# An encoder trunk on one core: every fourth low part of the weights made by ScalarE and an accumulating GpSimd DMA

## The chip, the cores and the metric

The kernel runs on one core of a Trainium2 chip. The metric is device microseconds of one execution; the median of two runs of the kernel before is 1818.07 us (1817.77 to 1818.36).

## What is computed

The reference is a trunk of two layers over 256 tokens of width 2048, all in float32. Cut to what matters:

```python
def hybrid_layer(x, ...):                       # x: (1, 256, 2048)
    h = rms_norm(x, norm_g)
    z = jnp.einsum('bsd,de->bse', h, w_in)      # 2048 -> 14848: q, k, v, gates of three branches, merge gates
    ya = retention(rq, rk, rv, ...)             # 4 heads of 256
    yb = multiscale_pool(pv, pool_w, ...)       # windows 2, 4, 8, 16
    yc = windowed_gqa(aq, ak, av, ...)          # 8 query heads, 2 key heads of 128
    ya, yb, yc = (y * silu(gate) @ w_branch)    # each 1024 -> 2048
    merged = g0 * ya + g1 * yb + g2 * yc
    return x + jnp.einsum('bsd,de->bse', merged, w_out)   # 2048 -> 2048
```

Nearly all arithmetic is in products of 256 tokens with weight matrices, 336 MB of weights in the two layers.

## The kernel before

The weights are cut into 628 tiles of 128 partitions x 1024 float32 (512 KB). `plan` lists them in the order of their use. To keep float32 precision with the faster float32r matmul, each weight tile is split into a high part (its value rounded to float32r) and a low part (the rest), and a product is the sum of three: high by high, high by low, low by high. A tile passes through these steps:

- SP loads it from HBM into a buffer `raw` (L193, four buffers).
- ScalarE (ACT) casts it to the high part `whi` (L200, four buffers).
- VectorE (DVE) subtracts: `wlo = raw - whi` (L207, three buffers).
- TensorE (PE) reads `whi` and `wlo`: `gemm_n` (L308, activations stationary, 12 matmuls of 512 columns a tile) or `gemm_t` (L338 and L341, weights stationary).

`weights()` is called once per tile and runs the steps ahead of the use: when tile i is taken, the low parts are issued up to tile i + 2, the high parts up to i + 3, and loads up to four tiles beyond the last low part. A buffer that is still read makes the instruction that refills it wait: the low part of tile j goes into the buffer of tile j - 3, so it waits for PE's last matmul on that low part; the load of tile j + 4 goes into the buffer of tile j, so it waits until both parts of tile j are made.

Beside this, `Side` runs the smaller work (norms, attention heads, retention, pooling, merge) as generators that advance by one tick per weight tile. They use ACT and DVE for what PSUM holds, PE for small products and transposes, and GpSimd (POOL) for 16 small powers (`rsqrt`, L382). PE's accumulators of a group of tiles are two PSUM buffers in turn. Within an engine the instructions run in the order in which the scheduler put them, and a waiting instruction holds all behind it on its engine; SP's loads are such a queue too.

Of the kernel before, what the change touches and what calls it, by code (L numbers as in the profile page):

```python
# [9 lines left out]
F32 = mybir.dt.float32  # L10
F32R = mybir.dt.float32r
AF = mybir.ActivationFunctionType
# [22 lines left out]


class Side:
    """Work beside the weight loops: generators that advance by one tick per weight tile; each yields the ticks to wait."""

    def __init__(self):  # L40
        self.live = []
# [25 lines left out]


class First(Task):
    """A task made on demand, apart from the ticks."""  # L70


@with_exitstack
def kernel(
# [71 lines left out]
            yield 1  # L146
        return task.value

# [1 line left out]
    def n_tiles(mat, c0, nk):  # L150
        return [(mat[k2 * 256:(k2 + 1) * 256, c0:c0 + 512].rearrange("(k p) e -> p k e", p=P), 2, 512) for k2 in range(nk // 2)]

# [50 lines left out]
    def lo_to(n):  # L203
        while len(los) < min(n, len(plan)):
            i = len(los)
            lo = wp.tile(list(raws[i].shape), F32R, tag="wlo", name=nm("wlo"), bufs=N_LO)
            nc.vector.tensor_sub(lo, raws[i], his[i].bitcast(F32))  # L207
            los.append(lo)

    def weights():  # L210
        """the next tile of the plan, split; splits and loads of later ones run ahead."""
        i = used[0]
        used[0] += 1
        ahead = min(i, 1) if i < 6 else N_LO - 1
        hi_to(i + ahead + 1)
        lo_to(i + ahead + 1)
        load_to(len(los) + N_RAW)
        hi_to(i + ahead + (1 if ahead < N_LO - 1 else 2))
        return his[i], los[i]

# [1 line left out]
    xa = cp.tile([P, 2, D], F32, name="xa")  # L222
    xr = x.rearrange("b (t p) d -> p (b t) d", p=P)

# [59 lines left out]
        yield 1  # L284
        nc.vector.tensor_copy(cols[:, 32:48], pc[:, 0:16])

# [1 line left out]
    def split(dst_hi, dst_lo, src, scale=None):  # L288
        if scale is None:
            nc.scalar.copy(dst_hi, src)  # L290
# [3 lines left out]
            nc.vector.scalar_tensor_tensor(dst_lo, src, scale, dst_hi.bitcast(F32), ALU.mult, ALU.subtract)  # L294

    def gemm_n(act, nk, early=False):
        """act [K, tokens] in split pairs of K-tiles; returns [tokens, 512]."""
        pt = acc("pn")
        n2 = nk // 2
        kept = []  # L300

        def products(k2, a2, hi, lo, t):
            ts = slice(t * P, (t + 1) * P)
            order = [(kk, ai, w) for kk in range(2) for ai, w in ((0, hi), (0, lo), (1, hi))]
            if k2 == 0:
                order.sort(key=lambda o: o[2] is lo)
            for n, (kk, ai, w) in enumerate(order):
                nc.tensor.matmul(pt[:, t, :], lhsT=a2[:, kk, ai, ts], rhs=w[:, kk], start=k2 == 0 and n == 0, stop=k2 == n2 - 1 and n == 5)  # L308

        for k2 in range(n2):  # L310
            a2 = need(act[k2])
            hi, lo = weights()
            if k2 + 1 < n2 and isinstance(act[k2 + 1], First):
                need(act[k2 + 1])
            products(k2, a2, hi, lo, 0)
            if early and k2 >= n2 - 2:
                kept.append((k2, a2, hi, lo, 1))
            else:
                products(k2, a2, hi, lo, 1)
            if k2 + 1 < n2:  # L320
                tick()
        for args in kept:
            products(*args)
        return pt

    def gemm_t(act):
        """returns psum of 256 channels as (p, 2): the sum of its two halves [tokens], unscaled."""
        pt = acc("pt")
        for k4 in range(KD // 4):
            hi, lo = weights()  # L330
            for kk in range(4):
                k = k4 * 4 + kk
                a = need(act[k // 2])[:, k % 2]
                for e in range(2):
                    es = slice(e * P, (e + 1) * P)

                    def big(start, stop):
                        nc.tensor.matmul(pt[:, e, :], lhsT=hi[:, kk, es], rhs=a.rearrange("p h n -> p (h n)"), start=start, stop=stop)  # L338

                    def small():  # L340
                        nc.tensor.matmul(pt[:, e, 0:S], lhsT=lo[:, kk, es], rhs=a[:, 0, :], start=False, stop=False)  # L341

                    if k == 0:
                        big(True, False)
                        small()
                    else:
                        small()
                        big(False, k == KD - 1)
            if k4 + 1 < KD // 4:
                tick()  # L350
        return pt

    def summed(pt):
        """the halves of gemm_t's result summed: [p, 2, tokens] in SBUF, and the scratch used."""
        b = half([P, 2, S], "tb")
        nc.scalar.copy(b, pt[:, :, S:2 * S])  # L356
        yield 1
        s = half([P, 2, S], "ts")
        nc.vector.tensor_add(s, pt[:, :, 0:S], b)
        return s, b  # L360

    def transposed(blocks, s):
        """blocks: 4 [128, 128] fp32 tiles -> psum bank [128, 512]."""
        pt = mix(s)
        for i, b in enumerate(blocks):
            nc.tensor.transpose(pt[:, i * P:(i + 1) * P], b, ident)  # L366
        return pt

    def mm3(ps, a, b, first, last):
        """ps += a.T @ b of (hi, lo) pairs."""  # L370
        nc.tensor.matmul(ps, lhsT=a[0], rhs=b[0], start=first, stop=False)  # L371
        nc.tensor.matmul(ps, lhsT=a[0], rhs=b[1], start=False, stop=False)  # L372
        nc.tensor.matmul(ps, lhsT=a[1], rhs=b[0], start=False, stop=last)  # L373

    def split_t(pt, s):
        """psum bank of 2 x 256 columns -> split pair of K-tiles."""
        o = slot([P, 2, 2, S], F32R, s)
        split(o[:, :, 0, :], o[:, :, 1, :], pt.rearrange("p (i n) -> p i n", i=2))
        return o
# [5 lines left out]
        return transposed([xa[:, t, (k2 * 2 + i) * P:(k2 * 2 + i + 1) * P] for i in range(2) for t in range(2)], "pht")  # L385

    def ht_split(l, k2, pt):
        """hT tile of columns 256 k2.. of x times the norm gain."""
        ht = slot([P, 2, 2, S], F32R, "ht")
        for i in range(2):  # L390
            nc.scalar.activation(ht[:, i, 0, :], pt[:, i * S:(i + 1) * S], AF.Copy, scale=g_col(l, k2 * 2 + i))  # L391
        for i in range(2):
            nc.vector.scalar_tensor_tensor(ht[:, i, 1, :], pt[:, i * S:(i + 1) * S], g_col(l, k2 * 2 + i), ht[:, i, 0, :].bitcast(F32), ALU.mult, ALU.subtract)  # L393
        return ht
# [13 lines left out]
        yield  # L408

    def scales_task(ss):  # L410
        """per-token norm scales: as columns and as a broadcast row."""
        yield 1
        st = tiny([P, 2], "st")
        nc.vector.reduce_sum(st, ss, axis=AX.X)
# [42 lines left out]
    for l in range(DEPTH):  # L457
# [3 lines left out]
            return tok["rstd"][:, t:t + 1]  # L461

        def gate_task(pt):
            """silu of a gate path from gemm_t."""
            s, sg = yield from summed(pt)
            nc.vector.tensor_tensor(s, s, tok["rbc"][:, None, :].to_broadcast([P, 2, S]), ALU.mult)
            nc.scalar.activation(sg, s, AF.Sigmoid)
            yield 1
            o = held([P, 2, S], "silu")
            nc.vector.tensor_tensor(o, s, sg, ALU.mult)  # L470
            return o

# [1 line left out]
        def qk_task(pt, nh, which):  # L474
            """RMS norm, gain and rotary of [tokens, nh heads] from psum; returns split transposes of head pairs."""
            sq = slot([P, 2, nh, AD], F32, "sq")
            src = pt[:, :, 0:nh * AD]
            nc.scalar.activation(sq.rearrange("p t h d -> p t (h d)"), src, AF.Square)
# [56 lines left out]
        akt, av = need(ak)[0], need(av)  # L535
        aqt = need(aq[0]) + need(aq[1])

# [1 line left out]
        def decay_task():  # L539
            lg = slot([P, 2, 2, S], F32, "lag")  # L540
            nc.sync.dma_start(out=lg, in_=c_lag)
# [15 lines left out]

        dms_task = start(decay_task())

# [1 line left out]
        scale = AD ** -0.5  # L561

        def attend_task(h, ut):
# [40 lines left out]
                ut.append(slot([P, 2, 2, S], F32R, "uta"))  # L604
            split(ut[h // 2][:, h % 2, 0, :], ut[h // 2][:, h % 2, 1, :], o)

# [1 line left out]
        def rot_task(pt):  # L608
            s, b = yield from summed(pt)
            ta = half([P, 2, S], "ta")  # L610
# [33 lines left out]
            tick()  # L644
            scts.append(start(scores_task(h, qt, kt)))

# [1 line left out]
        def rv_task(pt, outs):  # L648
            yield 1
            for t in range(2):  # L650
# [57 lines left out]
            tick()  # L708
            ut_ret += [start(retain_task(2 * j + i, rg_t)) for i in range(2)]

# [1 line left out]
        def pooled_task(g, pt):  # L712
            s, _ = yield from summed(pt)
            yield 1
# [40 lines left out]
            return ut  # L755

        def pool_out(g2):
            """groups 2 g2 and 2 g2 + 1."""
            hi, lo = weights()
            tasks = []  # L760
            for gi in range(2):
                g = 2 * g2 + gi
                p = need(pools[g])
                py = mix("py")
                for e in range(2):
                    es = slice(e * P, (e + 1) * P)
                    for dt in range(2):
                        r = gi * 2 + dt
                        mm3(py[:, e * S:(e + 1) * S], (hi[:, r, es], lo[:, r, es]), (p[:, dt, 0, :], p[:, dt, 1, :]), dt == 0, dt == 1)
                need(pgt[g])  # L770
                tasks.append(start(pool_out_task(g, py)))
            tick()
            return tasks
# [8 lines left out]
            if g == 2:  # L782
                ut_pool += pool_out(0)

# [1 line left out]
        def merge_task(b, c, pt, gs):  # L786
            yield 1
            if b == 0:
# [33 lines left out]
                if b == 2:  # L822
                    mt_tiles += [start(turn_task(c, j, merge_t)) for j in range(2)]

# [1 line left out]
        last = l + 1 == DEPTH  # L826
        if not last:
            ss = per_layer([P, 2, 4], "ss")
# [44 lines left out]


def _constants():
    """Tables that depend on the shapes alone."""
    import numpy as np

    f = np.float32
# [42 lines left out]
```

## Time and profile before

| | before |
|---|---|
| median of the runs | 1818.07 us |
| span of the profiled execution | 1816.5 us |
| PE busy | 1805.3 us (99%) |
| DVE busy | 1105.8 us (61%) |
| ACT busy | 856.5 us (47%) |
| POOL busy | 19.0 us (1%) |
| raw loads on SP's queue | 335.94 MB, 61.1% of the DMA engines' span |

The profiled execution's own time is its span of 1816.5 us, from the first to the last instruction; the median of the runs is 1.6 us above it. Engines work side by side, so the busy times do not add up. A busy share says how loaded an engine is; whether it sets the end is seen in the chain of waits, which is followed back from the last instruction. Line numbers are those of the kernel before; behind L207 those of the changed kernel are 4 higher.

### The profile page before, as it was taken

To read this page: it belongs to the slowest core of one execution; us is meant where nothing else is said; L and a number is where in the kernel's file an instruction comes from. 1 tells how busy PE (TensorE), PEld (TensorE's weight loads), DVE (VectorE), ACT (ScalarE), POOL (GpSimd) and SP (SyncE) were. 2 spreads that over 40 slices of the span, in tenths; PEclk is the share of its full clock that TensorE was granted. 3 is DMA by queue.
4 is the path that set the end of the run, shared out by engine and by line. 5 is a ranking of instruction groups with operands and counts; after the bars stand their busy time and mean duration, and the time that the engine had idled before them with its cause. 6 is when DMAs were issued, how large, how long until landed. Compare 5 with 4: busy or idle time off the path is not lost.

```text
span 1816.5 us, 23260 instructions
## 1 busy us (share of the span) xinstructions
PE 1805.3 (99%) x8882; PEld 1522.3 (84%) x8882; DVE 1105.8 (61%) x1354; ACT 856.5 (47%) x1087; POOL 19.0 (1%) x22
## 2 busy tenths in 40 slices
PE   8999999999999999999999999999999999999998
PEld 6888888888888888888888888888888888888887
DVE  6678865676544545555567787657754454555554
ACT  6456554445444444444444555544444444444442
POOL 0000000000000000000000000000000000000000
PEclk9999999999999999999999999999999999999999
DMA  7665556566666666665566655565666666666664
GB/s 266 183 199 164 153 169 186 163 187 191 191 196 196 191 194 196 185 186 186 185 187 185 194 162 154 172 179 171 186 190 194 196 186 198 195 192 188 188 201 147
DMA packets 217087, 337.43 MB, mean 186 GB/s; under 512 B 10848, under 2 KB 95760, under 8 KB 216976
## 3 DMA queue, kind: packets, MB, share of 16 engines
q1 hardware_dynamic: 216928, 335.94, 61.1%
q8 instruction: 69, 1.13, 0.3%
q14 instruction: 42, 0.34, 0.1%
q10 hardware_dynamic: 48, 0.02, 0.0%
HBM read 333.82 MB, written 2.10 MB: 185 GB/s over the span
## 4 chain that ended last, share of the span: by engine, by line
PE 98%; DMA 1%; ACT 0%; DVE 0%; issue 0%; SPq 0%; DVEq 0%; ACTq 0%
PE pn L308 69%; PE pt L338 16%; PE pt L341 8%; DMA raw<-in_w_in_dram 0%; PE pmt L366 0%; PE ppt L366 0%; DMA dec<-in_ret_decay_bwd_dram 0%; PE pht L366 0%; PE pqt L366 0%; ACT whi L200 0%; PE pro L373 0%; PE py L373 0%; PE pss L373 0%; PE py L372 0%; PE psc L373 0%; PE pss L371 0%
## 5 line engine op out<-in xcount | busy, mean ns | idle before, releaser
L207 DVE TENSOR_TENSOR wlo<-raw,whi 128x1024 fp32r<-128x1024 f32 x628 | 768.9, 1224 | 627.5 <-PE pn L308 498.0
L200 ACT CAST whi<-raw 128x1024 fp32r<-128x1024 f32 x628 | 661.4, 1053 | 763.4 <-PE pn L308 575.3
L308 PE MATMUL pn<-whi,ht 128*128 128x512 f32 x2432 | 754.1, 391 | 1.0 <-ACT ht L391 0.7
L308 PEld LDWEIGHTS pn<-whi,ht 128*128 128x128 f32 x2432 | 456.8, 188 | 96.5 <-DVE ht L393 1.2
L308 PE MATMUL pn<-wlo,ht 128*128 128x512 f32 x1216 | 461.6, 390 | 0.0
L338 PE MATMUL pt<-ht,whi 128*128 128x512 f32 x1280 | 450.3, 397 | 0.0
L341 PE MATMUL pt<-ht,wlo 128*128 128x256 f32 x1280 | 353.2, 281 | 0.0
L338 PEld LDWEIGHTS pt<-ht,whi 128*128 128x128 f32 x1280 | 238.9, 188 | 53.1
L308 PEld LDWEIGHTS pn<-wlo,ht 128*128 128x128 f32 x1216 | 228.7, 188 | 46.5
L341 PEld LDWEIGHTS pt<-ht,wlo 128*128 128x128 f32 x1280 | 241.5, 189 | 2.9
L308 PE MATMUL pn<-whi,mt 128*128 128x512 f32 x512 | 158.2, 391 | 0.0
L308 PEld LDWEIGHTS pn<-whi,mt 128*128 128x128 f32 x512 | 96.1, 188 | 19.8
L308 PE MATMUL pn<-wlo,mt 128*128 128x512 f32 x256 | 97.0, 389 | 0.0
L308 PE MATMUL pn<-whi,uta 128*128 128x512 f32 x256 | 77.6, 389 | 0.0
L308 PE MATMUL pn<-whi,utr 128*128 128x512 f32 x256 | 77.5, 389 | 0.0
L308 PE MATMUL pn<-whi,utp 128*128 128x512 f32 x256 | 77.5, 389 | 0.0
L308 PEld LDWEIGHTS pn<-whi,utp 128*128 128x128 f32 x256 | 48.0, 188 | 10.0
L308 PEld LDWEIGHTS pn<-whi,utr 128*128 128x128 f32 x256 | 48.1, 188 | 9.9
L308 PEld LDWEIGHTS pn<-wlo,mt 128*128 128x128 f32 x256 | 48.1, 188 | 9.8
L308 PEld LDWEIGHTS pn<-whi,uta 128*128 128x128 f32 x256 | 47.9, 188 | 9.9
L356 ACT COPY tb<-pt 128x512 f32<-128x512 f32 x40 | 23.4, 585 | 54.7 <-PE pt L338 54.5
L815 ACT ACTIVATE mg<-pn,rstd 128x512 f32<-128x512 f32 x48 | 30.4, 686 | 39.4 <-PE pn L308 39.4
(154 smaller groups left out, 1091.6 us busy)
## 6 DMA issues: line engine op xcount, KB each, us to landing
raw<-in_w_in_dram SPq DMA_DIRECT2D x464, 512.0 KB, 3.7
raw<-in_w_out_dram SPq DMA_DIRECT2D x64, 512.0 KB, 4.3
raw<-in_w_att_dram SPq DMA_DIRECT2D x32, 512.0 KB, 3.7
raw<-in_w_ret_dram SPq DMA_DIRECT2D x32, 512.0 KB, 4.6
raw<-in_w_pool_dram SPq DMA_DIRECT2D x32, 512.0 KB, 4.5
raw<-in_pool_w_dram SPq DMA_DIRECT2D x4, 512.0 KB, 3.9
out_dram<-o SPq DMA_DIRECT2D x8, 256.0 KB, 5.5
xa<-in_x_dram SPq DMA_DIRECT2D x3, 512.0 KB, 8.1
```

Of the source, the lines that this page charges most:

```text
L200: nc.scalar.copy(hi, raws[i])
L207: nc.vector.tensor_sub(lo, raws[i], his[i].bitcast(F32))
L308: nc.tensor.matmul(pt[:, t, :], lhsT=a2[:, kk, ai, ts], rhs=w[:, kk], start=k2 == 0 and n == 0, stop=k2 == n2 - 1 and n == 5)
L338: nc.tensor.matmul(pt[:, e, :], lhsT=hi[:, kk, es], rhs=a.rearrange("p h n -> p (h n)"), start=start, stop=stop)
L341: nc.tensor.matmul(pt[:, e, 0:S], lhsT=lo[:, kk, es], rhs=a[:, 0, :], start=False, stop=False)
L356: nc.scalar.copy(b, pt[:, :, S:2 * S])
L815: nc.scalar.activation(g, pt[:, t], AF.Sigmoid, scale=sc(t))
```

## The change

For every tile with an index of 12 or more whose remainder by four is 1 (154 of 628), the low part is no longer made by DVE. ScalarE writes the tile, scaled by -1 and rounded to float32r, into the buffer of the low part. That is the negated high part, made from `raw` and not from `whi`. Then GpSimd issues a DMA from `raw` to that buffer which adds what it reads to what stands there: -high + raw. The other 474 tiles are as before. Comments are left out of the diff.

```diff
         while len(los) < min(n, len(plan)):
             i = len(los)
             lo = wp.tile(list(raws[i].shape), F32R, tag="wlo", name=nm("wlo"), bufs=N_LO)
-            nc.vector.tensor_sub(lo, raws[i], his[i].bitcast(F32))
+            if i >= 12 and i % 4 == 1:
+                nc.scalar.activation(lo, raws[i], AF.Copy, scale=-1.0)
+                nc.gpsimd.dma_start(out=lo.bitcast(F32), in_=raws[i], accum_op=ALU.add)
+            else:
+                nc.vector.tensor_sub(lo, raws[i], his[i].bitcast(F32))
             los.append(lo)
```

Where the instructions stand now is seen on ACT, in the output projection of the second layer. A name is the buffer with the number of its tile; `whi` is a high part, `wlo` a low part. Before:

```order
L200 CAST whi_14273<-raw_14214 128x1024
L200 CAST whi_14291<-raw_14235 128x1024
L200 CAST whi_14315<-raw_14253 128x1024
L200 CAST whi_14333<-raw_14271 128x1024
L200 CAST whi_14351<-raw_14289 128x1024
L200 CAST whi_14369<-raw_14313 128x1024
L200 CAST whi_14387<-raw_14331 128x1024
L200 CAST whi_14405<-raw_14349 128x1024
```

After the change, at the same tiles' place:

```order
L200 CAST whi_14421<-raw_14362 128x1024
L208 ACTIVATE wlo_14435<-raw_14362 128x1024
L200 CAST whi_14440<-raw_14383 128x1024
L200 CAST whi_14464<-raw_14401 128x1024
L200 CAST whi_14482<-raw_14419 128x1024
L200 CAST whi_14500<-raw_14438 128x1024
L208 ACTIVATE wlo_14514<-raw_14438 128x1024
L200 CAST whi_14519<-raw_14462 128x1024
```

The negated copy (L208) has come in behind the high part of the same tile and ahead of the high part of the next. It waits for PE's last matmul on the low part of three tiles before.

The other place on ACT is where the gates are taken out of PSUM (`mg`, L815 before, L819 now). Before:

```order
L815 ACTIVATE mg_5582<-pn_5433,rstd_423 128x512
L815 ACTIVATE mg_5584<-pn_5433,rstd_423 128x512
L200 CAST whi_5591<-raw_5530 128x1024
L200 CAST whi_5609<-raw_5548 128x1024
L200 CAST whi_5627<-raw_5566 128x1024
L200 CAST whi_5645<-raw_5589 128x1024
```

After:

```order
L819 ACTIVATE mg_5634<-pn_5483,rstd_423 128x512
L819 ACTIVATE mg_5636<-pn_5483,rstd_423 128x512
L200 CAST whi_5643<-raw_5582 128x1024
L200 CAST whi_5662<-raw_5600 128x1024
L208 ACTIVATE wlo_5657<-raw_5582 128x1024
L200 CAST whi_5680<-raw_5618 128x1024
L200 CAST whi_5698<-raw_5641 128x1024
```

Here the copy for raw_5582 stands behind the high part of the next tile (raw_5600) as well. The first pattern holds for 121 of the 154 copies, this one for 33.

On SP, the queue of the loads, at the end of the program, with the semaphores that each waits for (DMAHW: a load or store, DMASW: a GpSimd transfer). Before:

```order
L193 DMA raw_14481<-in_w_out_dram 128x2x512 [waits DMAHW3_49,DVE_49]
L193 DMA raw_14499<-in_w_out_dram 128x2x512 [waits DMAHW4_49,DVE_49]
L193 DMA raw_14517<-in_w_out_dram 128x2x512 [waits DMAHW5_49,DVE_49]
L193 DMA raw_14535<-in_w_out_dram 128x2x512 [waits DMAHW6_49,DVE_49]
L193 DMA raw_14553<-in_w_out_dram 128x2x512 [waits DMAHW1_49,DVE_49]
```

After:

```order
L193 DMA raw_14614<-in_w_out_dram 128x2x512 [waits DMAHW1_49,DMASW6_49]
L193 DMA raw_14632<-in_w_out_dram 128x2x512 [waits DMAHW3_49,DVE_49]
L193 DMA raw_14650<-in_w_out_dram 128x2x512 [waits DMAHW4_49,DVE_49]
L193 DMA raw_14669<-in_w_out_dram 128x2x512 [waits DMAHW0_49,DVE_49]
L193 DMA raw_14687<-in_w_out_dram 128x2x512 [waits DMAHW5_49,DMASW7_49]
```

One load in four now waits for a GpSimd transfer (DMASW) where it waited for DVE, and those behind it on SP wait with it.

## Rows read from the trace of the kernel before

**Rows 1.** The page's parts 1 and 2: span, busy time by engine, granted clock by slice.
```profile
span 1816.5 us, 23260 instructions
...
PE 1805.3 (99%) x8882; PEld 1522.3 (84%) x8882; DVE 1105.8 (61%) x1354; ACT 856.5 (47%) x1087; POOL 19.0 (1%) x22
...
PEclk9999999999999999999999999999999999999999
```

**Rows 2.** The page's part 4, chain that ended last, share of the span by engine.
```profile
PE 98%; DMA 1%; ACT 0%; DVE 0%; issue 0%; SPq 0%; DVEq 0%; ACTq 0%
```

**Rows 3.** Groups by line: operation, shapes, count | busy us, mean ns | idle before, releaser.
```profile
L207 DVE TENSOR_TENSOR wlo<-raw,whi 128x1024 fp32r<-128x1024 f32 x628 | 768.9, 1224 | 627.5 <-PE pn L308 498.0
...
L200 ACT CAST whi<-raw 128x1024 fp32r<-128x1024 f32 x628 | 661.4, 1053 | 763.4 <-PE pn L308 575.3 <-PE pt L338 100.3 <-issue 33.2
...
L478 ACT ACTIVATE sq<-pn 128x1024 f32<-128x1024 f32 x4 | 4.1, 1028 | 6.7 <-PE pn L308 6.7
```

**Rows 4.** Timeline of a steady stretch, 499 to 508 us: start us, us, engine, line, operation.
```profile
501.36 0.39 PE L308 MATMUL pn<-wlo,ht 128*128 128x512 f32 x1
501.36 0.41 PEld L308 LDWEIGHTS pn<-whi,ht 128*128 128x128 f32 x2
...
501.84 1.22 DVE L207 TENSOR_TENSOR wlo<-raw,whi 128x1024 fp32r<-128x1024 f32 x1 [1.49 <-PE pn L308]
502.01 1.06 ACT L200 CAST whi<-raw 128x1024 fp32r<-128x1024 f32 x1 [1.66 <-PE pn L308]
502.04 0.39 PE L308 MATMUL pn<-wlo,ht 128*128 128x512 f32 x1
...
504.56 1.23 DVE L207 TENSOR_TENSOR wlo<-raw,whi 128x1024 fp32r<-128x1024 f32 x1 [1.50 <-PE pn L308]
...
507.28 1.23 DVE L207 TENSOR_TENSOR wlo<-raw,whi 128x1024 fp32r<-128x1024 f32 x1 [1.50 <-PE pn L308]
...
507.48 0.39 PE L308 MATMUL pn<-wlo,ht 128*128 128x512 f32 x1
507.48 0.41 PEld L308 LDWEIGHTS pn<-whi,ht 128*128 128x128 f32 x2
```

**Rows 5.** DMA: the load queue, its loads of 512 KB (last column us to landing), landing of L193.
```profile
q1 hardware_dynamic: 216928, 335.94, 61.1%
...
raw<-in_w_in_dram SPq DMA_DIRECT2D x464, 512.0 KB, 3.7
...
raw<-in_w_ret_dram SPq DMA_DIRECT2D x32, 512.0 KB, 4.6
...
lag<-in_c_lag_dram SPq DMA_DIRECT2D x2, 512.0 KB, 5.3
...
DMA to landing us min/median/max: 3.4/3.7/9.0
```

**Rows 6.** Busy time by stage: PE, PEld, DVE, ACT, POOL, then granted clock, DMA share, GB/s.
```profile
core 0: us, PE busy (x) PEld busy (x) DVE busy (x) ACT busy (x) POOL busy (x), PEclk, DMA share, GB/s
5.00:10.00 5.00, 3.88 (x13) 2.75 (x12) 3.43 (x7) 3.54 (x6) 0.00 (x0) 1.00 1.02 374
10.00:20.00 10.00, 10.00 (x50) 8.23 (x49) 6.44 (x9) 6.95 (x14) 0.00 (x0) 1.00 1.04 374
30.00:34.00 4.00, 3.12 (x13) 1.97 (x12) 3.56 (x5) 4.00 (x10) 0.00 (x0) 1.00 0.34 99
760.00:800.00 40.00, 40.00 (x185) 33.09 (x185) 22.31 (x23) 17.84 (x20) 0.00 (x0) 1.00 0.62 185
```

**Rows 7.** Line L382, the small GpSimd instructions: duration ns min/median/max.
```profile
L382 POOL TENSOR_TENSOR rr<-m,nhalf x8: 695/697/1127, 311.5 to 1244.8; 128x2 f32<-128x2 f32 x8
...
L382 POOL TENSOR_TENSOR rstd<-ms,nhalf x2: 695/702/710, 38.0 to 918.6; 128x2 f32<-128x2 f32 x2
```

**Rows 8.** Waits of SP's DMA queue: waited for, us in total, times, longest us.
```profile
SPq L193 <- DVE wlo L207: 1433.2, 598, 5.9
```

More of the change, by code (lines that the diff above doesn't have):

```diff
@@ L69 @@
 class First(Task):
+    pass
 @with_exitstack
```

## The prediction

> **What bounds the kernel now.** I read the busy shares first: PE 1805.3 us of a span of 1816.5, at a granted clock of 1.00 in every slice, which is the upper of its two levels (2.4 GHz) [rows 1]. The chain of waits says the same: 98% of the chain that ended last is PE, DVE and ACT are at 0% [rows 2]. So the kernel is bound by its matmuls, and all that is not PE is worth at most 1816.5 - 1805.3 = 11.2 us. VectorE's subtraction for the low part is the costliest DVE group (628 x 1.224 us), ScalarE's cast for the high part the costliest ACT group (628 x 1.053 us), and both spend more idle time in front of these groups waiting for PE to give a buffer back [rows 3]. They are ahead of PE, not behind it. How far ahead is read from the timeline of a steady stretch [rows 4]: PE's last matmul on a low tile starts at 501.36 and lasts 0.39, DVE's next subtraction starts at 501.84 (a handoff of 0.09) and recurs every 2.72 us (501.84, 504.56, 507.28). That is PE's time for a tile.
>
> **The slack the change draws on.** Three wlo buffers turn. The buffer that DVE refills at 501.84 is for the tile two ahead, whose first matmul on a low part stands at 507.48 [rows 4]. So from the release of a buffer to its need there are 507.48 - 501.84 = 5.64 us. DVE uses 1.22 of them and leaves 4.42. Beside weight tiles PE does other matmuls: 1816.5/628 = 2.89 us for a tile on average against 2.72 in the steady stretch, 0.69 us in four tiles. Half of it, 0.35, falls on average in the two tiles of this window and lengthens it.
>
> **Removed.** 154 of 628 subtractions leave DVE: 154 x 1.224 = 188 us, 1106 to 917 busy. DVE is not on the chain, its idle time in front of those rows ends with PE, and a shorter DVE releases nothing that PE waits for: worth 0. The most it could give is a share of the 11.2 us above.
>
> **Added, on ACT.** 154 scaled copies of 128x1024. This form is not in the trace; the cast of that shape takes 1.053, the square of that shape 1.028 [rows 3], so 1.05. ACT goes from 857 to 857 + 162 = 1019 us, half of the longer span: it does not become the bound. What is queued behind a copy on ACT is the high part of a later tile and the evacuations of PSUM. The high part stands three tiles ahead of its use, and the matmul groups alternate between two PSUM accumulators, so that an evacuation has a group of 4 or 8 tiles (11 us or more) as cover: 0. Without that cover each of 154 would cost up to 1.05.
>
> In 121 of 154 cases the order puts the negated copy right behind the high part of the same tile; in 33 also behind the high part of the next one, which waits for a release of PE that comes at about the same time (502.01 against 501.84 in [rows 4]) and lasts 1.06. I charge those 33 with 1.06 each, 35 us, once the slack is used up.
>
> **Added, on POOL and the DMA engines.** 154 accumulating transfers of 512 KB from SBUF to SBUF, issued by GpSimd. No row of the trace has one, or any GpSimd transfer. Call X the time from its issue to its landing. The chain for such a tile is copy 1.05, handoff 0.09, X, against a window of 5.64 + 0.35. PE waits X + 1.14 - 5.99 = X - 4.85 for each. Everything hangs on X.
>
> Bounds of X. Below: a plain load of the same size lands 3.7 us after issue (median, minimum 3.4) [rows 5]; the low end is 3.7. Above: the slowest raw load took 9.0 [rows 5], at the start, when the DMA engines' share was 1.02 to 1.04 [rows 6]; the high end is 9.0. Between them I build X from three rows.
> - A load with company: medians run from 3.7 (w_in) to 4.6 (w_ret) [rows 5]. The accumulate runs while raw loads run (share 0.62 in a steady stretch [rows 6]); middle, 4.1.
> - A second pass: the transfer has to read its destination as well as its source. One pass of 512 KB costs 61.1% x 1816.5 / 640 = 1.73 us of all 16 engines (335.94 MB on q1 is 640 such loads) [rows 5]. Add 1.73.
> - GpSimd issues in software: the shortest of its L382 instructions, 128x2 elements, takes 0.70 [rows 7]; I take that for making the transfer's list. Add 0.70.
>
> X = 4.1 + 1.73 + 0.70 = 6.53. It lies about midway between the ends; I would sooner err upwards, since a pass is known to cost and nothing speaks for a saving.
>
> A page of the Trainium skill speaks for a lower X: "DMA: Bandwidth & Descriptors", section "Anatomy of one DMA — SWDGE (gpsimd) path", gives a fixed 2.0 us plus the bytes at 436 GB/s for a transfer issued by GpSimd. That would be an estimate of 3.2 us for 512 KB, and 4.4 us if a second pass at the same rate is added; by either, PE would hardly wait and the time would be that of the first rival below. The rows here are longer for the plain load (3.7 against 3.2), and no run here shows a GpSimd transfer.
>
> **Moved, on SP.** The raw buffer of such a tile is given back by the landing, not by DVE. SP waits in order; now it waits 1433 us in 598 waits for DVE's subtraction and is that far from being late [rows 8]. After the change the load of the tile four ahead is issued at the landing, and the next two or three loads behind it go out in a burst. The circle through that buffer is copy 1.05, handoff 0.09, X, load L, handoff 0.09, cast 1.05, handoff 0.09: X + L + 2.4. The circle through the wlo buffer is copy 1.05, handoff 0.09, X, and PE from the first use to the release of the next tile's buffer, 507.28 - 502.04 = 5.24 [rows 4]: X + 6.4. They are level at L = 4.0, so at 3.7 the load is just hidden. Cost 0, with no cover to spare.
>
> On POOL 16 small instructions (L382) now stand in one queue with transfers that wait for ACT. Their readers come a tick, one tile, later: 2.72 us of cover; 0, at most 16 x 2.72 = 44.
>
> **Sum.** 154 x (6.53 - 4.85) = 259, plus 35, is 294 us. 1816.5 + 294 = 2110.5; the median of the runs lies 1.6 above the profiled span (1818.07 - 1816.5), so 2112 us, a factor of 1.16.
>
> **Rivals.**
> - *The transfer stays hidden (not slower).* Place: the window of 5.64 + 0.35. If X is under 4.85, PE waits only behind the 33 later copies. At X = 4.4 that is 33 x (4.4 - 3.79) = 20 us, 1838 us; at 3.7 nothing, 1818. It decides at X = 4.9, where 33 x 1.06 + 154 x 0.05 reaches the 36 us that are 2%. For it: SBUF on both sides, 4.42 us of slack now. Against it: one more pass than the load that alone takes 3.7.
> - *The load behind it becomes the bound.* If raw loads in a burst, sharing the engines with the accumulate, land after 5.3 us, as the 512 KB of the lag table do [rows 5], the raw circle is 1.3 longer than the wlo circle: 154 x 1.3 = 200 us more, about 2310. The same region is reached by an X of 7.8. For it: the two circles are level at L = 4.0, and the engines' share rises from 61% to (0.611 x 1816.5 + 154 x 3.46)/2112 = 78%. Against it: SP's first load after the landing meets an empty queue.
> - *The granted clock falls.* PE now never stops long; with a gap in every fourth tile the clock could drop to its lower level. If it ran the next tile at half rate, 154 x 2.72 = 419 more, 2531. Against it: between 30 and 34 us PE was busy 3.12 of 4.00 us and the granted clock stayed at 1.00 [rows 6].
> - *Faster by over 2%.* DVE's 188 us would have to be on PE's path; the 11.2 us above forbid it.
>
> That the change does not do what it says is excluded: the order has 154 copies, 154 transfers and 474 subtractions.
>
> **How the numbers follow.** X between 4.9 and 7.5, the forecast, 1855 to about 2260: 0.60. Hidden: 0.12. Load or a larger X, above 2260: 0.24. Clock: 0.03. Faster: 0.01. A measurement of this kernel tells about 2% from no change. So slower by over 2%: 0.87, same 0.12, faster 0.01. The range leaves out most of the hidden case below and the largest X (above 8.7) and the clock above: 1845 to 2450. The likeliest case's own range is 1855 to 2260.
>
> **What would show it.** Right: a GpSimd queue with 154 x 0.5 MB; PE idle in front of matmuls on wlo with the transfer as releaser, 154 waits of some 1.7 us; a distance of about 12.6 us (10.88 + 1.68) between such tiles in a steady stretch; issue to landing of the transfer near 6.5; DVE near 917 and ACT near 1019 us busy; granted clock 1.00. Landing below 4.9 and no PE waits: the first rival. PE waits for ACT's cast and that for a raw load: the second. A granted clock below 1.00 in steady slices: the third. The forecast is wrong above all if X is not what three rows of other work make of it.

## The result: slower by a factor of 1.071, 129 us instead of the 294 forecast

The changed kernel takes 1947.34 us (two runs, 1945.5 to 1949.17) against 1818.07 before: a ratio of 1.071, 95% interval 1.0693 to 1.0728. The direction and the place were as forecast and the time lies inside the range, but the loss is 0.44 of the one predicted: 129 us and not 294.

The page of the changed kernel answers [rows 1], [rows 2] and [rows 5]. Its first lines are the span, the busy time by engine and the granted clock by slice, then the two queues that carry the weights (packets, MB, share of the 16 DMA engines' span) and the chain that ended last by engine:

```profile
span 1947.4 us, 23591 instructions
...
PE 1848.8 (95%) x8882; PEld 1521.0 (78%) x8882; DVE 924.9 (47%) x1200; ACT 999.5 (51%) x1241; POOL 151.4 (8%) x176
...
PEclk9999999999999999999999999999999999999999
...
q1 hardware_dynamic: 216928, 335.94, 53.9%
q0 software_dynamic: 22176, 80.75, 23.5%
...
PE 49%; DMA 31%; issue 12%; ACT 4%; DVE 3%; POOL 0%; SPq 0%; POOLq 0%; DVEq 0%; ACTq 0%
```

In [rows 2] the chain was PE for 98%; now PE is on it for 49% and DMA for 31%. PE is idle for 1947.4 - 1848.8 = 98.6 us, 87 more than the 11.2 of before, and its busy time has grown by 43.5 us with the same 8882 matmuls. Together they are the 131 us by which the span grew, and most of both comes from one event, as the next two views show. The waits name the releaser (engine, line, waited for, us in total, times, longest):

```profile
PEld pn L312 <- DMA wlo<-raw: 112.6, 100, 5.3
...
PE pn L312 <- DMA wlo<-raw: 71.7, 94, 4.9
...
PEld pt L345 <- DMA wlo<-raw: 22.5, 25, 1.6
...
PE pt L345 <- DMA wlo<-raw: 14.8, 21, 1.3
```

The rows of PEld are weight loads that wait at the same time, so only the rows of PE are added: 71.7 + 14.8 = 86.5 us of PE's idle time end with the landing of a GpSimd transfer; there is no such row before. The timeline of one tile shows the whole chain that the prediction put together (start us, us, engine, line, operation, idle before and its releaser); it answers [rows 4]:

```profile
564.37 0.39 PE L312 MATMUL pn<-wlo,ht 128*128 128x512 f32 x1
...
564.80 1.06 ACT L208 ACTIVATE wlo<-raw 128x1024 fp32r<-128x1024 f32 x1 [1.40 <-PE pn L312]
...
566.15 0.86 POOL L209 DMA_DIRECT2D wlo<-raw  x1 [10.70 <-ACT wlo L208]
...
570.04 0.61 PE L312 MATMUL pn<-whi,ht 128*128 128x512 f32 x2
...
570.93 0.19 PEld L312 LDWEIGHTS pn<-wlo,ht 128*128 128x128 f32 x1 [0.70 <-DMA wlo<-raw]
570.93 0.50 PE L312 MATMUL pn<-wlo,ht 128*128 128x512 f32 x1 [0.28 <-DMA wlo<-raw]
```

PE's last matmul on the low part of three tiles before ends at 564.76, the copy starts at 564.80 and ends at 565.86, GpSimd starts 0.29 us later, and PE's first matmul on that low part starts at 570.93, as soon as the transfer has landed, 4.78 us after its issue. In [rows 4] PE's last matmul on a low part ends at 501.75 and the need stands at 507.48, 5.73 us later. Counted like this from 564.76 the window ends at 570.49: 0.44 us are lost. Only 0.28 of them show as idle time, since matmuls that do not wait overlap (the one before ends at 570.65), and the matmul after the wait shows 0.50 us instead of the 0.39 of [rows 4]. So part of the loss stands in PE's busy time. The duration of the transfer is on the page of its line:

```profile
L209 POOL DMA_DIRECT2D wlo<-raw x154: 859/859/1050, 45.1 to 1929.5; - x154
...
DMA to landing us min/median/max: 4.5/4.8/7.0
```

The median is 4.8, where the prediction had built 6.53.

### The profile page after: what moved, and what is told of

It reads as the page before. It is cut to its first block, busy times and chain, and to the rows that moved or that the text cites. A ratio compares the mean times of both kernels' runs of the same rounds, so it can differ in the third digit from the quotient of the medians.

```text
span 1947.4 us, 23591 instructions
## 1 busy us (share of the span) xinstructions
PE 1848.8 (95%) x8882; PEld 1521.0 (78%) x8882; DVE 924.9 (47%) x1200; ACT 999.5 (51%) x1241; POOL 151.4 (8%) x176
## 3 DMA queue, kind: packets, MB, share of 16 engines
q0 software_dynamic: 22176, 80.75, 23.5%
q8 instruction: 69, 1.13, 0.3%
## 4 chain that ended last, share of the span: by engine, by line
PE 49%; DMA 31%; issue 12%; ACT 4%; DVE 3%; POOL 0%; SPq 0%; POOLq 0%; DVEq 0%; ACTq 0%
PE pn L312 30%; DMA wlo<-raw 24%; PE pt L342 10%; PE pt L345 5%; ACT wlo L208 4%; DMA raw<-in_w_in_dram 3%; DVE wlo L211 2%; DMA raw<-in_w_out_dram 1%; DMA raw<-in_w_att_dram 1%; DMA raw<-in_w_pool_dram 1%; DMA raw<-in_w_ret_dram 1%; ACT whi L200 0%; DMA dec<-in_ret_decay_bwd_dram 0%; PE ppt L370 0%; DMA xa<-in_x_dram 0%
## 5 line engine op out<-in xcount | busy, mean ns | idle before, releaser
L211 DVE TENSOR_TENSOR wlo<-raw,whi 128x1024 fp32r<-128x1024 f32 x474 | 580.5, 1225 | 870.5 <-PE pn L312 685.0
L312 PE MATMUL pn<-wlo,ht 128*128 128x512 f32 x1216 | 470.9, 397 | 41.8 <-DMA wlo<-raw 41.6
L345 PE MATMUL pt<-ht,wlo 128*128 128x256 f32 x1280 | 355.5, 283 | 14.9 <-DMA wlo<-raw 14.8
L209 POOL DMA_DIRECT2D wlo<-raw x154 | 133.2, 865 | 1647.5 <-ACT wlo L208 1525.8
L208 ACT ACTIVATE wlo<-raw 128x1024 fp32r<-128x1024 f32 x154 | 162.9, 1058 | 142.6 <-PE pn L312 108.4
L312 PEld LDWEIGHTS pn<-wlo,mt 128*128 128x128 f32 x256 | 48.1, 188 | 23.2 <-DMA wlo<-raw 13.8
L312 PE MATMUL pn<-wlo,utp 128*128 128x512 f32 x128 | 48.6, 400 | 8.4 <-DMA wlo<-raw 8.4
```

Of the source, the lines that this page charges most:

```text
L208: nc.scalar.activation(lo, raws[i], AF.Copy, scale=-1.0)
L209: nc.gpsimd.dma_start(out=lo.bitcast(F32), in_=raws[i], accum_op=ALU.add)
```

## The experiments

Eight kernels, each the changed kernel with the edit shown, timed beside the kernel before (1818.3 us in both sets).

**The second pass alone.** The transfer becomes a plain copy; the addition is left out, and the low part of these tiles is `raw` itself.

```diff
-                nc.gpsimd.dma_start(out=lo.bitcast(F32), in_=raws[i], accum_op=ALU.add)
+                nc.gpsimd.dma_start(out=lo.bitcast(F32), in_=raws[i])
```

> The transfer is a plain copy from raw to wlo (no accumulate), all waits and orders kept; the low part of every fourth tile is then raw itself, so a part of the result is left wrong. Theory A (the second read runs beside the first and is cheap in latency): issue to landing 4.3 to 4.8 us instead of 4.79, time 1900 to 1947 us; by shifting each tile's stall in the trace of the changed kernel, 0.2 us less is 1922 us, 0.5 us less 1890 us. Theory B (the second pass costs its own engine time in latency: 23.5% x 1947 / 154 = 2.97 us against 53.9% x 1947 / 640 = 1.64 us for a load, 1.33 us): landing 3.4 to 3.5 us, time about 1830 us. Both: occupancy of the transfer falls from 2.97 to about 1.6 us of the 16 engines.

Measured 1829.71 us, ratio 1.0062 (1.0047 to 1.0077). The queue's share of the 16 engines, on the page:

```profile
q0 software_dynamic: 22176, 80.75, 11.1%
```

GpSimd's instruction (ns min/median/max) and the landing, on the view of its line, and PE's largest row of waits for the transfer (us in total, times, longest):

```profile
L209 POOL DMA_DIRECT2D wlo<-raw x154: 527/527/711, 44.9 to 1811.5; - x154
...
DMA to landing us min/median/max: 2.8/2.9/5.5
```

```profile
PE pn L312 <- DMA wlo<-raw: 4.8, 5, 3.6
```

The theory of a pass that runs beside the first (A) is refuted. That of a pass with its own price (B) holds in kind and in time; the landing came out 0.5 us below what it expected, and the engines' share at 1.32 us where it had 1.6. The landing falls by 4.79 - 2.90 = 1.89 us: the engines' share per transfer from 23.5% x 1947.4 / 154 = 2.97 us to 11.1% x 1828.9 / 154 = 1.32, 1.65 less, and GpSimd's instruction by 0.33. In the traces the first packet starts 1.43 us after the issue with the add and 1.09 without, so those 0.33 us are part of the latency. The term of 1.73 us in the sum was about right: 1.65 in the engines. What was wrong is in the rest: the plain transfer lands in 2.9 us, where the sum had 4.1 + 0.70 = 4.8.

**Software queue against hardware queue.** The same plain copy, issued by ScalarE; here too the addition is left out.

```diff
-                nc.gpsimd.dma_start(out=lo.bitcast(F32), in_=raws[i], accum_op=ALU.add)
+                nc.scalar.dma_start(out=lo.bitcast(F32), in_=raws[i])
```

> The same plain copy issued by ScalarE's hardware queue instead of GpSimd (again the low part of every fourth tile is raw itself). If GpSimd's 0.86 us for building the list is part of the latency, the landing is 0.86 - 0.37 = 0.5 us or more below that of the plain GpSimd copy, and the handoff of 0.29 us to GpSimd is gone as well: time 40 to 80 us below that of the plain GpSimd copy, or at most 1830 us. If the software queue costs nothing, landing and time are those of the plain GpSimd copy within 0.1 us and 1%.

Measured 1822.43 us, ratio 1.0022 (1.0013 to 1.0031). The same view of the line:

```profile
L209 ACTq DMA_DIRECT2D wlo<-raw x154: 472/472/511, 44.6 to 1803.9; - x154
...
DMA to landing us min/median/max: 2.9/2.9/6.4
```

The landing is 2.9 us from either queue. The issue rows, 0.53 and 0.47 us, differ by 0.06. The time fits both expectations, the landing only the second. So the 0.70 us charged for GpSimd's software was not there in a plain transfer. 7 us in time remain between the two runs. Most of them are one tile (465): with GpSimd's queue its transfer was issued 2.88 us after the copy, PE waited 3.6 us for it, until 1374.6, and the granted clock stood at 0.50 from 1374.2 to 1377.6. What is left is within what the handoff of 0.29 us to GpSimd, gone here, can account for; that was not tried by itself.

**ScalarE's part alone.** No transfer; DVE adds.

```diff
-                nc.gpsimd.dma_start(out=lo.bitcast(F32), in_=raws[i], accum_op=ALU.add)
+                nc.vector.tensor_tensor(lo, raws[i], lo.bitcast(F32), ALU.add)
```

> No GpSimd transfer: ScalarE writes the negated copy as in the change, and VectorE adds raw to it in place. All 154 copies on ScalarE stay where they stand. If the time comes from PE waiting for the transfer, the chain is 1.06 + 0.06 + 1.23 us, well inside 5.64 us, and the time is 1815 to 1830 us. If it comes from the 163 us of extra work on ScalarE and from what is queued behind the copies, most of the 129 us stays: 1900 us or more.

Measured 1818.43 us, ratio 1.0001 (0.9991 to 1.001). Busy time by engine, on the page:

```profile
PE 1805.3 (99%) x8882; PEld 1522.6 (84%) x8882; DVE 1105.1 (61%) x1354; ACT 1000.8 (55%) x1241; POOL 18.1 (1%) x22
```

All 154 copies are on ScalarE, where the change put them, ScalarE is as busy as in the changed kernel (1000.8 and 999.5 us), and PE's busy time is that of before to a tenth. The work on ScalarE and what is queued behind it cost nothing as long as the chain ends well inside the window.

**A longer window.** The transferred low parts get a buffer of their own.

```diff
-N_SLOTS = 25
+N_SLOTS = 24
...
-            lo = wp.tile(list(raws[i].shape), F32R, tag="wlo", name=nm("wlo"), bufs=N_LO)
+            own = i >= 12 and i % 4 == 1
+            lo = wp.tile(list(raws[i].shape), F32R, tag="wla" if own else "wlo", name=nm("wlo"), bufs=1 if own else N_LO)
```

> The low parts that the transfer makes get a buffer of their own (one, so that it is free one tile earlier), paid for by one of the 25 slots of the smaller work. The transfer, its duration and its bytes stay. If the 129 us are the window of 5.64 us between release and need being too short by about 0.5 us, the window is now 2.7 us longer, the stalls at the first matmul on such a low part vanish, the clock does not drop, and the time is 1815 to 1835 us. If the transfers slow the loads (the raw buffer's circle) or the DMA engines' load of 77% is the cause, the time stays above 1880 us.

Measured 1837.32 us, ratio 1.01 (1.0083 to 1.0117). Of the 129 us, 110 go, with the same transfers and the same bytes: the short window was their cause. 19 us stay, 2 us over the expectation. What stays is read from three rows of waits (us in total, times, longest) and from the issue row of the transfer (KB each, median us to landing):

```profile
ACT wlo L209 <- DMA raw<-in_w_in_dram: 149.9, 52, 4.2
...
PEld pn L313 <- DMA wlo<-raw: 18.3, 26, 2.6
...
PE pn L313 <- DMA wlo<-raw: 8.5, 12, 2.2
```

```profile
wlo<-raw POOLq DMA_DIRECT2D x154, 512.0 KB, 5.5
```

The copy is now released so early that it waits for the raw load, and the transfer takes 5.5 us instead of 4.8. So there are two candidates: the circle through the raw buffer, and the loads that share the DMA engines with the transfer. The trace has both. By the starts of the matmuls, 24 tiles wait, 16.6 us in all; at 21 of them (13.8 us) the copy had waited for its raw load, and at the 24 the transfer took 6.5 us on average against 5.5 at the others. The last run below takes the first candidate away.

**Half the bytes.**

```diff
-                nc.scalar.activation(lo, raws[i], AF.Copy, scale=-1.0)
-                nc.gpsimd.dma_start(out=lo.bitcast(F32), in_=raws[i], accum_op=ALU.add)
+                k = raws[i].shape[1] // 2
+                nc.vector.tensor_sub(lo[:, 0:k], raws[i][:, 0:k], his[i][:, 0:k].bitcast(F32))
+                nc.scalar.activation(lo[:, k:], raws[i][:, k:], AF.Copy, scale=-1.0)
+                nc.gpsimd.dma_start(out=lo[:, k:].bitcast(F32), in_=raws[i][:, k:], accum_op=ALU.add)
```

> In the tiles of the change the first half of the columns stays with VectorE's subtraction, and only the second half is copied by ScalarE and added by GpSimd's transfer: 256 KB instead of 512. If the landing grows with the bytes (the accumulate took 2.97 us of the 16 engines, 4.79 us from issue to landing), half the bytes land 1.3 to 1.5 us sooner, at 3.3 to 3.5 us; the copy takes 0.62 instead of 1.06. The chain is then 0.22 + 0.62 + 0.30 + 3.4 = 4.5 us against the window of 5.64, and the time is 1818 to 1830 us. If the landing is a fixed latency that hardly depends on the bytes, it stays above 4.3 us, the chain is 5.5 us or more, and the time is 1840 to 1880 us.

Measured 1819.57 us, ratio 1.0008 (0.9999 to 1.0017). The issue row (KB each, median us to landing):

```profile
wlo<-raw POOLq DMA_DIRECT2D x154, 256.0 KB, 3.3
```

PE's busy time, on the page:

```profile
PE 1805.8 (99%) x8882; PEld 1522.3 (84%) x8882; DVE 1025.1 (56%) x1354; ACT 936.2 (52%) x1241; POOL 152.1 (8%) x176
```

256 KB land in 3.3 us, 512 KB in 4.8: the latency grows with the bytes, 1.5 us for 256 KB. With a copy of 0.63 us the chain is 0.63 + 0.29 + 3.3 = 4.2 us and fits the 5.64; PE no longer waits: 1817.7 - 1805.8 = 11.9 us idle, as before. The accumulating transfer as such costs nothing once its chain is inside the window.

**A fifth raw buffer.** One slot is given for it.

```diff
-N_RAW, N_HI, N_LO = 4, 4, 3
-N_SLOTS = 25
+N_RAW, N_HI, N_LO = 5, 4, 3
+N_SLOTS = 24
```

> The changed kernel with a fifth raw buffer and loads issued one tile further ahead, paid for by one of the 25 slots of the smaller work. If the wlo buffer's window sets PE's waits, a load that starts one tile sooner helps nothing: 1930 to 1950 us, VectorE's and ScalarE's waits for loads small as before. If the circle through the raw buffer (copy, transfer, load, cast) is what PE waits for, the 129 us go, to 1840 us or less.

Measured 1940.4 us, ratio 1.0681 (1.0663 to 1.0699), the same within half a per cent as the change itself. PE's larger row of waits for the transfer, 71.7 us in the changed kernel:

```profile
PE pn L312 <- DMA wlo<-raw: 65.1, 91, 3.2
```

The second rival, the load behind the transfer, is not what PE waits for. The run also gives a slot away, as the run with the own buffer does, and the time does not rise; that the fifth buffer pays for a loss by the slot is not excluded.

**One tile in eight.**

```diff
-            if i >= 12 and i % 4 == 1:
+            if i >= 12 and i % 8 == 1:
```

> The transfer for one tile in eight (77 instead of 154). If each transfer costs PE its own wait at one tile, the excess is half: 1818 + 65 = 1883 us, 1870 to 1890. If the excess comes from what the transfers do together (the DMA engines' load of 77%, loads pushed into bursts), it falls to a quarter or less: 1850 us or below.

Measured 1871.01 us, ratio 1.029 (1.0275 to 1.0305). 77 transfers cost 52.7 us, 0.68 each; 154 cost 129, 0.84 each. Most of the price is each transfer's own, at its own tile; about a fifth comes from their number. By the starts of the matmuls, these 77 tiles wait 46 us here and 53 in the changed kernel, and the granted clock, which falls four times in the middle of the changed kernel (see below), does not fall here.

**Both buffers.** The own buffer and the fifth raw buffer together, for two slots (`N_SLOTS = 23`).

> The own buffer for the transferred low parts (1837 us by itself) together with a fifth raw buffer, paid for by two of the 25 slots. In the run with the own buffer alone ScalarE's copies waited 247 us in 83 waits for raw loads, and PE still 37 us for transfers. If what was left there, 19 us, is the circle through the raw buffer, the fifth buffer takes it away: 1818 to 1825 us. If what was left is the load on the DMA engines, it stays at 1830 to 1840 us.

Measured 1860.08 us, ratio 1.0224 (1.0209 to 1.0239): outside both expectations, slower than the own buffer alone by 23 us. The waits of PE's weight loads and matmuls for the transfer, that of SP's queue, and the issue row:

```profile
PEld pn L313 <- DMA wlo<-raw: 38.7, 43, 2.4
...
PE pn L313 <- DMA wlo<-raw: 21.5, 32, 1.9
```

```profile
SPq L193 <- DMA wlo<-raw: 1177.1, 152, 10.7
```

```profile
wlo<-raw POOLq DMA_DIRECT2D x154, 512.0 KB, 6.2
```

ScalarE's copies hardly wait for loads any more (2.1 us in one wait), so the raw circle is open, and still PE waits more. SP's wait for landings is not what has changed: 341.5 us in the changed kernel, it is 1130.8 with the own buffer alone already. What has changed is the company of the transfers. Counted in the traces, 0.65 raw loads are under way on average while a transfer is in the changed kernel, 0.81 with the own buffer, 1.01 with both; the median landings are 4.8, 5.5 and 6.2 us. Within this run, the half of the transfers with the least company (0.72 loads) lands after 5.7 us on average, the half with the most (1.31) after 7.3. So the fifth buffer does not give back the 19 us of the own buffer, and the expectation that it would is refuted; it is not shown that the raw circle had no part in them, since the copies that waited for loads stand at most of the waits there. That company on the DMA engines makes the transfers later is borne out by these counts, but no run here takes the company away by itself. (The 37 us that the expectation gives for PE's waits add weight loads and matmuls, which wait at the same time; the matmuls alone waited 12.6.)

## Why the prediction was wrong in size and right in place

*What bounds the kernel, and the slack.* Right. PE was the bound. That the window sets the loss is shown by the run with the own buffer, which lengthens it by a tile, and its length by all 154 tiles: from PE's release to the first use, less the stall, it averages 6.00 us. Counted like this from the end of PE's matmul, [rows 4] has 5.73, so the cover by other matmuls is 0.27, where the forecast had 0.35.

*Removed from DVE: worth 0.* Right. DVE fell to 924.9 us (917 forecast) and nothing was gained; with the 154 subtractions back on DVE and ScalarE's copies left in, the time is that of before.

*Added on ACT: 0 and 35 us.* Right, nearly in size too. The copies took 1.06 us (1.05); ScalarE was busy for 999.5 us, where 1019 were forecast. The 33 copies behind the next high part started 0.78 us after the release of their buffer on average, the other 121 after 0.07. At the 33 tiles PE lost 46 us, at the 121 it lost 61: 0.89 us more each, 29 us where 35 were charged.

*X, the step that failed.* The sum of three terms was 6.53 us; the median is 4.79, the mean 4.89.
- Second pass: 1.73 forecast, 1.89 measured by the plain copy, of which 1.65 in the engines. The term was right, and it decides whether the chain fits: without it the loss is 11 us. That it is the second read which costs, and not the adding, is not shown: no run here separates the two. A page of the Trainium skill, "Collectives: The Full Stack", section "The bandwidth ceiling: the fold count and why AG ≠ RS ≠ AR", says of a ring's ReduceScatter that it is slower than AllGather, which copies, because the add needs two source reads, not because the add costs cycles. The times here agree with that: 2.97 us of the engines with the add, 1.32 without.
- Base: 4.1 forecast, 2.9 measured. The row taken for it was a load from HBM with company, with 3.7 to 4.6 us. A transfer from SBUF to SBUF of the same size lands 0.8 us before the fastest of these medians. The two differ in more than the endpoints: most of a load's packets are of 1 or 2 KB, the transfer's of 4 KB. No run here separates these.
- Software: 0.70 forecast, none measured in a plain transfer: 2.9 us from both queues. With the add GpSimd's instruction is 0.33 us longer; that stands in the 1.89 above. The row taken for the term was a GpSimd instruction of another kind.

The page of the Trainium skill that I set aside, "DMA: Bandwidth & Descriptors", "Anatomy of one DMA — SWDGE (gpsimd) path", gave an estimate of 3.2 us for the plain transfer and of 4.4 with a second pass. The runs gave 2.9 and 4.8. As a size it was nearer than my rows. As a verdict it was not: at 4.4 us my own formula gave 1838 us.

*The sum.* Worked again with the measured means over all 154 tiles: lateness 0.22, copy 1.06, handoff 0.31, transfer 4.89, start of the matmul 0.04, together 6.52 against the window of 6.00. That is 0.52 x 154 = 80 us. The forecast had 7.90 against 5.99, 1.91 x 154 = 294. So X took 1.64 x 154 = 253 us out, and the handoff to GpSimd, taken from a row of PE and DVE as 0.09, was 0.22 too short: 34 us the other way. Two more things the sum did not have. The tiles are not alike: 32 of 154 do not wait, and the 27 us of slack that they have left are of no use to the others. That makes 107 us at the first matmuls on a transferred low part (122 waits of 0.88 us on average, where 154 of some 1.7 were forecast; worked out from the starts of the matmuls). And what follows a wait: a matmul 0.11 us longer in most cases, 14 us in all, and the clock, about 8.5. Together that is 129 of the 131 us by which the span grew.

*The load, SP and POOL.* Right for the change: a fifth raw buffer moved little. GpSimd's 16 small instructions in one queue with the transfers were charged with 0; three of the 154 transfers were issued more than 0.33 us after their copy. The latest, at tile 465, came after 2.25 us, with no releaser in the profile, and took 7.0 us to land; PE lost 4.9 us there. The same tile is as late in the runs with the own buffer, with half the bytes, with a fifth raw buffer and with both buffers (2.25 us), so it belongs to the program. Why it comes so late stays open.

*The rivals.* Hidden: it decides at X = 4.9, said the text (its formula reaches 36 us at 4.86), and at the measured 4.79 the formula gives 33 x 1.0 = 33 us, 1851 us. The formula was too kind by the terms above, and it takes all transfers as alike: the plain copy at a median of 2.9 us still loses 11 us, nearly all at the few tiles whose transfer took 4 us or more or was issued late. The threshold of 2% lies between 2.9 and 4.8, not at 4.9. The load as bound: refuted. Faster: as excluded.

*The clock* was held for a rival with 0.03 and happened on a small scale. The granted clock of the changed kernel, by stage (the columns of [rows 6]):

```profile
core 0: us, PE busy (x) PEld busy (x) DVE busy (x) ACT busy (x) POOL busy (x), PEclk, DMA share, GB/s
610.00:620.60 10.60, 8.35 (x37) 6.57 (x35) 3.51 (x3) 6.31 (x7) 0.86 (x1) 1.00 0.75 191
...
622.08:625.49 3.41, 3.41 (x9) 2.65 (x9) 1.30 (x2) 0.89 (x1) 0.00 (x0) 0.50 0.84 299
625.49:640.00 14.51, 13.43 (x59) 10.74 (x59) 6.00 (x7) 5.46 (x7) 0.86 (x1) 1.00 0.70 183
...
1465.90:1472.00 6.10, 6.06 (x14) 4.79 (x15) 1.23 (x1) 0.92 (x1) 0.00 (x0) 0.50 0.52 172
```

PE waited 2.30 us up to 620.65, and from 622.08 to 625.49 the clock was at 0.50, the lower of its two levels (1.2 GHz). In all there were four such stretches in the middle of the kernel, 17 us together; at half the clock that is about 8.5 us lost. Three followed waits of 2.3, 3.2 and 2.1 us, the fourth began inside that of 4.9; the short waits of most tiles left the clock at 1.00, and one of 2.6 us did too. The forecast's row for this, a clock of 1.00 over 0.9 us of idle time in [rows 6], was true and did not reach so far.

## What to carry to other kernels

Where a new operation's only price is whether its latency fits a window, write down the window, every handoff in the chain and the latency as separate terms, and look for the row that is like the new operation in its endpoints and its packets: a load from HBM was no measure for a copy inside SBUF (3.7 against 2.9 us). Check also how alike the cases are: here 33 of 154 tiles hold 46 of the 107 us of waiting. Relief for an engine that is not on the chain is worth nothing, and here it was paid for with a chain of three engines in place of one subtraction that ran 4.4 us early. If such work must move, make its chain shorter (half the bytes: 1819.6 us) or its window longer (a buffer of its own: 1837.3 us); neither beats the kernel before, since PE's 1805 us stay.

## What the runs showed of the hardware that was not expected

- A copy of 512 KB inside SBUF lands 2.9 us after issue from GpSimd's software queue and from ScalarE's hardware queue alike; the issue rows take 0.53 and 0.47 us.
- With the add, the same transfer lands after 4.8 us, takes 2.97 instead of 1.32 us of the 16 DMA engines, and GpSimd's issue takes 0.86 us instead of 0.53.
- From the end of ScalarE's copy to the start of GpSimd's instruction pass 0.29 us, where PE's end to DVE's start took 0.09 in [rows 4].
- More buffers can make a transfer later: with an own buffer, and then with a fifth raw buffer as well, its median landing went from 4.8 to 5.5 and 6.2 us, while the raw loads under way beside it went from 0.65 to 0.81 and 1.01 on average.
- The first packet of the transfer starts 1.43 us after the issue with the add, 1.09 without it, and 1.13 from ScalarE's queue.
